# Interleaving the two halves of every moving operand in a two-block transformer kernel

## The chip, the cores and the metric

The kernel runs on one core of a Trainium2 chip. The metric is the device time of one execution in microseconds (us). The engines that matter here are TensorE (PE in the profile, with PEld for its weight loads), VectorE (DVE), ScalarE (ACT), GpSimd (POOL) and SyncE (SP), which issues the transfers.

## What is computed

Two transformer blocks in a row act on one sequence of 256 tokens of width 2048, all in float32. The first block has two kinds of attention and a feed-forward part with a short convolution:

```python
h = rmsnorm(x, pre_mix_g)
proj = h @ w_in                                   # 2048 -> 4368
o_a = swa_sink_attention(q_a, k_a, v_a, sinks)    # 16 heads, 2 kv heads, window 128
o_b = forgetting_attention(q_b, k_b, v_b, log_f)  # 16 heads
mix = concat(rmsnorm(o_a), rmsnorm(o_b)) @ w_out  # 2048 -> 2048
x = x + rmsnorm(mix, post_mix_g)
u = causal_dwconv(rmsnorm(x, pre_ffn_g) @ w_up, conv_w, conv_b)   # 2048 -> 11264, 3 taps
gate, val = split(u, 2)
x = x + rmsnorm((gelu(gate) * val) @ w_down, post_ffn_g)          # 5632 -> 2048
```

The second block modulates its norms by a condition vector (`w_ada`, 2048 to 12288), projects the sequence and a context of 256 tokens, runs windowed attention and pooling, and ends with `square(relu(hm @ w_mlp_up)) @ w_mlp_down` (2048 to 8192 and back) and a last norm. The weights, some 485 MB by the page's HBM reads, are read once.

## The kernel before

Every product of activations and weights is made of three matmuls. A weight tile arrives by DMA (`raw`), ACT copies it to a rounded part `hi` (line 160), DVE writes the remainder `lo = raw - hi` (line 172), and the activations are held as `hi` and `lo` in the same way. `products` (line 294) then issues hi·hi, hi·lo and lo·hi into one PSUM bank.

Two shapes of matmul carry nearly all the work. In form A the weights are the stationary operand (128 columns) and the transposed activations x^T are the moving operand, 256 columns: the output has features on the partitions. The groups v (first part), kva, qa, qk, q, up and mup read x^T that `make_ht` has written into tiles of `xt_tile` (line 367), 192 bytes past the start of a tile of 8,448 bytes. In form B the activations are stationary and 512 columns of weights move (groups wo_a, wo_b, wo_p, dn, mdn, u; 352 and 336 columns in v; 256 in kv and ckv). Counted over the program, line 294 issues 9,312 matmuls of 256 columns, 3,552 of 512 and 288 of 352 or 336.

A group is one weight matrix slice: `run` walks its blocks, each of two half-blocks. A half-block is 24 matmuls of 256 columns or 12 of 512. `hi` and `lo` have four tiles each, so ACT and DVE can be at most four half-blocks ahead. Other DVE and ACT work is written between half-blocks, at `tick`: the reading of finished PSUM banks (`after`), attention (`sides`), and the sums over `w_ada` (`fill`). The order on each engine is then set by the scheduler of the framework from this text. After an up group, `taps` reads the banks for the convolution: one ACT and two DVE instructions for each of 8 slices of 256 columns, spread over the ticks of the group that follows. Groups run up0, up1, up2, then dn (both halves), up3, up4, dn and so on; later mup and mdn alternate.

Two kinds of extra matmul stand in the program. `LEAD` names 15 groups in which one short matmul (64 rows, 128 columns, line 289) goes ahead of a block's first product; its output is overwritten or not used. `warm_mix` (line 344) fills TensorE while the norm between two parts is worked out by ACT and DVE, ahead of up0 and of mup0: five matmuls each of several read patterns of one operand, all with 512 columns: in a row (`plain`), every second column, two halves in turn (`turns(2)`, columns 0, 256, 1, 257, ...), four parts 128 columns apart in turn (`turns(4)`, also 512), and others.

Of the kernel before, what the change touches and what calls it, by code (L numbers as in the profile page):

```python
# [9 lines left out]
F32R = mybir.dt.float32r  # L10
# [62 lines left out]
class Kernel:  # L73
# [204 lines left out]
    def products(self, bank, prog, w, x, first, last):  # L278
        nc = self.nc
        (wh, wl), (xh, xl) = w, x  # L280
        for n, op in enumerate(prog):
            passes = ((wh, xh), (wh, xl), (wl, xh))
            for m, (ww, xx) in enumerate(passes):
# [7 lines left out]
                else:  # L291
                    _, o, w_, tt, c = op
                    dst, lhsT, rhs = bank[:, o:o + w_], xx[:, 128 * tt:128 * tt + 128], ww[:, c:c + w_]
# [35 lines left out]
    def warm_mix(self, kind, after, x):  # L329

        bk = self.bank("warm")
        x = x.rearrange("p k t -> p (k t)")
        one = self.ones.bitcast(mybir.dt.bfloat16)
        plain, every2, every4 = x[:, 0:512], x[:, 0:1024:2], x[:, 0:2048:4]
        turns = lambda n: x[:, 0:512].rearrange("p (a b) -> p b a", a=n)
        w, flat = x[:, 1024:1152], x[:, 1024:1025].to_broadcast([128, 128])
        same = x[:, 0:2].rearrange("p (o n) -> p o n", o=1).broadcast_to([128, 256, 2])
        kinds = (((one[:, 0:128], one.rearrange("p (o n) -> p o n", o=1).broadcast_to([128, 2, 256])), (w, plain), (w, every2), (w, same), (flat, plain),
                  (w, turns(2))), ((w, every4), (w, turns(16)), (w, turns(4))))[kind]
        with self.tc.issue_after(after.ins):  # L340
            for lhsT, rhs in kinds:
                out = bk if len(rhs.shape) == 2 else bk.rearrange("p (a b) -> p a b", b=rhs.shape[-1])
                for _ in range(5):
                    self.pe.matmul(out, lhsT, rhs, start=True, stop=True, skip_group_check=True)
# [298 lines left out]
    def main(self):  # L643
# [82 lines left out]
        st = {}  # L726
# [3 lines left out]
        def v_after(banks):  # L730
            st["vb"] = vb = [self.P4([128, 1024]) for _ in range(2)]
            f = self.const("f", [128, 32])
            for tt in range(2):
                self.dve.tensor_tensor(out=f[:, 16 * tt:16 * tt + 16], in0=banks[3 * tt + 2][:, 320:336],
                                        in1=heads[:, 0:16], op=ALU.add)
            for tt in range(2):
                for c, w in enumerate((352, 352, 320)):
                    dst, src = vb[tt][:, 352 * c:352 * c + w], banks[3 * tt + c][:, 0:w]
                    if (tt + c) % 2:
                        self.dve.tensor_copy(out=dst, in_=src)  # L740
                    else:
                        ac.copy(dst, src)
# [51 lines left out]
        def kva_after(banks):  # L794
            st["kva"] = kva = self.P4([128, 1024])
            ac.copy(kva[:, 256:512], banks[0][:, 256:512])
            self.dve.tensor_copy(out=kva[:, 0:256], in_=banks[0][:, 0:256])
# [23 lines left out]
        def qa_after(banks):  # L821
            st["qa"] = qa = [self.P4([128, 4, 256]) for _ in range(2)]
            copy_out(pairs(qa), banks)
# [26 lines left out]
        def qk_group(part):  # L850
            def after(banks):
                st["qk", part] = qk = [self.P4([128, 4, 256]) for _ in range(2)]
                copy_out(pairs(qk), banks)
# [17 lines left out]
        def wo_a(half):  # L871
# [9 lines left out]
            def after(banks):  # L881
                for tt in range(2):
                    for c in range(2):
                        dst = st["m"][tt][:, 1024 * half + 512 * c:1024 * half + 512 * c + 512]
                        r = st["ra"][:, tt:tt + 1]
                        ac.activation(dst, banks[2 * tt + c], AF.Copy, scale=r)
# [35 lines left out]
        def wo_b(half):  # L922
# [11 lines left out]
            def done(n, bank):  # L934
# [3 lines left out]
                self.dve.scalar_tensor_tensor(out=m, in0=bank, scalar=st["rb"][:, tt:tt + 1], in1=m,  # L938
# [18 lines left out]
        def up(g):  # L957
            def after(banks):
# [4 lines left out]
                def taps(s, i):  # L963
                    if not gv:
# [30 lines left out]
        def accumulate(y, bank, n, half, first):  # L995
            tt, c = divmod(n, 2)
            d = y[tt][:, 1024 * half + 512 * c:1024 * half + 512 * c + 512]
            if first:
                ac.copy(d, bank)
# [529 lines left out]
```

## Time and profile before

| | us |
|---|---|
| median of 3 runs | 2121.12 |
| lowest, highest | 2119.36, 2122.55 |
| the profiled execution, own time | 2122.08 |
| its span from first to last instruction | 2120.3 |
| PE busy / DVE busy / ACT busy in it | 2096.9 / 1576.0 / 1079.0 |

Busy time of PE counts a matmul until its modelled end, and matmuls overlap, so 99% busy does not mean that PE streams at its best rate. The rate is the distance between the starts of matmuls that follow each other. In the chain of waits a piece such as "x864" is a stretch in which one matmul follows the other, and its time divided by its count is that distance.

### The profile page before, as it was taken

Reading aid. Unit: us, or ns where it says so; the run is one execution under the profiler, and the core shown is the slowest. Engines: PE = TensorE matmul, PEld = TensorE weight load, DVE = VectorE, ACT = ScalarE, POOL = GpSimd, SP = SyncE. Lnnn points to the kernel's source line nnn. Section 1 sums busy time; section 2 is a strip of 40 time slices with the busy share of each in tenths; the row PEclk is TensorE's granted clock in tenths of the full one; section 3 lists DMA queues with packets and bytes.
Section 4 is the critical chain, followed back from the end, with each engine's and each line's share of the span. In section 5 each row is a group of like instructions: output and inputs, shape, how many; then the busy total and the mean of one; then the engine's idle time right before and its main releaser. Section 6 shows DMA issues by size and latency. Waiting matters only on the chain.

```text
span 2120.3 us, 34973 instructions
## 1 busy us (share of the span) xinstructions
PE 2096.9 (99%) x14314; PEld 1902.6 (90%) x14314; DVE 1576.0 (74%) x2094; ACT 1079.0 (51%) x1557; POOL 40.3 (2%) x58
## 2 busy tenths in 40 slices
PE   8999999999999999999999999999999999999997
PEld 7998977999998999989989978889898998989986
DVE  6777688888678787897899788765656667555476
ACT  5446565555444553544566476454543434434343
POOL 0001000000000000000000000000000000000000
PEclk9999999999999999999999999999999999999999
DMA  8753576566667788787878754845667677555572
GB/s 308 270 185 138 154 222 240 213 250 233 257 235 263 254 295 307 283 316 277 303 278 276 275 174 144 218 159 181 248 211 275 207 262 249 193 199 183 196 238 100
DMA packets 120960, 491.39 MB, mean 232 GB/s; under 512 B 8736, under 2 KB 12640, under 8 KB 107360
## 3 DMA queue, kind: packets, MB, share of 16 engines
q1 hardware_dynamic: 120800, 489.16, 66.8%
q8 instruction: 112, 1.84, 0.3%
q14 instruction: 48, 0.39, 0.1%
HBM read 484.90 MB, written 2.13 MB: 230 GB/s over the span
## 4 chain that ended last, share of the span: by engine, by line
PE 94%; DVE 3%; DMA 1%; ACT 1%; issue 0%; POOL 0%; SPq 0%; POOLq 0%; ACTq 0%; DVEq 0%
PE b_up L294 23%; PE b_mup L294 17%; PE b_mdn L294 16%; PE b_dn L294 10%; PE b_qk L294 4%; PE b_wo_a L294 4%; PE b_v L294 2%; PE b_u L294 2%; PE b_wo_p L294 2%; PE b_qa L294 2%; PE b_q L294 2%; PE b_wo_b L294 2%; DVE lo L172 1%; PE b_aux L1228 1%; PE b_aux L1185 1%; PE b_aux L1214 1%
## 5 line engine op out<-in xcount | busy, mean ns | idle before, releaser
L172 DVE TENSOR_TENSOR lo<-raw,hi 128x1024 fp32r<-128x1024 f32 (+2 forms) x716 | 849.5, 1199 | 404.2 <-ACT hi L160 401.1
L160 ACT CAST hi<-raw 128x1024 fp32r<-128x1024 f32 (+2 forms) x716 | 731.2, 1031 | 816.1 <-PE b_up L294 206.7
L294 PE MATMUL b_up<-a,hi 128*128 128x256 f32 x2816 | 484.5, 277 | 0.0
L294 PEld LDWEIGHTS b_up<-a,hi 128*128 128x128 f32 x2816 | 425.3, 188 | 0.5
L294 PE MATMUL b_up<-a,lo 128*128 128x256 f32 x1408 | 390.1, 277 | 0.0
L294 PE MATMUL b_mup<-a,hi 128*128 128x256 f32 x2048 | 352.7, 278 | 1.2 <-ACT a L400 1.2
L294 PE MATMUL b_mdn<-hi,p 128*128 128x512 f32 x1024 | 315.5, 389 | 0.0
L294 PEld LDWEIGHTS b_mup<-a,hi 128*128 128x128 f32 x2048 | 309.0, 188 | 1.9 <-ACT a L400 1.5
L294 PE MATMUL b_mup<-a,lo 128*128 128x256 f32 x1024 | 283.5, 277 | 0.0
L294 PEld LDWEIGHTS b_up<-a,lo 128*128 128x128 f32 x1408 | 264.3, 188 | 0.1
L613 DVE SCALAR_TENSOR_TENSOR raw<-raw,srow 128x2048 f32<-128x2048 f32 x96 | 219.6, 2287 | 38.2 <-DMA raw<-in_w_ada 37.8
L294 PEld LDWEIGHTS b_mdn<-hi,p 128*128 128x128 f32 x1024 | 191.7, 188 | 39.4
L294 PE MATMUL b_dn<-hi,p 128*128 128x512 f32 x704 | 217.1, 390 | 0.0
L294 PE MATMUL b_mdn<-lo,p 128*128 128x512 f32 x512 | 199.2, 389 | 0.0
L294 PEld LDWEIGHTS b_mup<-a,lo 128*128 128x128 f32 x1024 | 193.0, 188 | 0.0
L294 PEld LDWEIGHTS b_dn<-hi,p 128*128 128x128 f32 x704 | 131.6, 188 | 26.9
L294 PE MATMUL b_dn<-lo,p 128*128 128x512 f32 x352 | 137.1, 390 | 0.0
L294 PEld LDWEIGHTS b_mdn<-lo,p 128*128 128x128 f32 x512 | 96.1, 188 | 20.0
L294 PE MATMUL b_qk<-a,hi 128*128 128x256 f32 x512 | 92.6, 283 | 0.0
L610 DVE SCALAR_TENSOR_TENSOR p<-raw,srow 128x2048 bf16<-128x2048 f32 x32 | 73.3, 2290 | 15.4 <-DMA raw<-in_w_ada 15.3
L294 PE MATMUL b_wo_a<-hi,a 128*128 128x512 f32 x256 | 80.3, 395 | 0.0
L294 PEld LDWEIGHTS b_qk<-a,hi 128*128 128x128 f32 x512 | 77.5, 188 | 2.8 <-issue 2.0
(276 smaller groups left out, 2527.4 us busy)
## 6 DMA issues: line engine op xcount, KB each, us to landing
raw<-in_w_ada SPq DMA_DIRECT2D x96, 1024.0 KB, 5.9
raw<-in_w_up SPq DMA_DIRECT2D x88, 1024.0 KB, 4.9
raw<-in_w_mlp_up SPq DMA_DIRECT2D x64, 1024.0 KB, 4.9
raw<-in_w_mlp_down SPq DMA_DIRECT2D x64, 1024.0 KB, 5.5
raw<-in_w_in SPq DMA_DIRECT2D x50, 1024.0 KB, 5.8
raw<-in_w_down SPq DMA_DIRECT2D x44, 1024.0 KB, 6.2
raw<-in_w_out SPq DMA_DIRECT2D x32, 512.0 KB, 6.7
raw<-in_w_out SPq DMA_DIRECT2D x16, 1024.0 KB, 6.6
```

The costliest lines, as they stand in the source:

```text
L160: nc.scalar.copy(h, r)
L172: self.dve.tensor_tensor(out=l, in0=r, in1=h.bitcast(F32), op=ALU.subtract)
L294: self.mm = self.pe.matmul(dst, lhsT, rhs, start=first and n == 0 and m == 0, stop=last and n == len(prog) - 1 and m == 2, skip_group_chec ...
L610: self.dve.scalar_tensor_tensor(out=junk, in0=r, scalar=1.0, in1=self.srow[1], op0=ALU.mult, op1=ALU.mult, accum_out=self.adac[:, f:f + 1])
L613: self.dve.scalar_tensor_tensor(out=r, in0=r, scalar=1.0, in1=self.srow[0], op0=ALU.mult, op1=ALU.mult, accum_out=self.ada[:, f:f + 1])
L1185: self.pe.matmul(bk.rearrange("p (m c) -> p m c", m=2), qq, k.rearrange("p (m c) -> p m c", m=2)[:, :, o:o + 256], start=n == 0, stop=n == ...
L1214: self.pe.transpose(bk[:, 128 * m:128 * m + 128], z[:, 128 * m:128 * m + 128], self.ident)
L1228: self.pe.matmul(o[64 * s:64 * s + 64, 128 * qt:128 * qt + 128], v[:, c:c + 64], PT[x][:, 128 * kt:128 * kt + 128], start=kt == 0, stop=kt ...
```

## The change

Every moving operand of `products` is read as two halves in turn: `halves` turns columns 0..n-1 into 0, n/2, 1, n/2+1, and so on. The output is written to PSUM in the order in which columns come (`turns` leaves it contiguous), so a bank now holds its columns interleaved. Whoever reads a bank puts them back by reading every second element (`evens`, `evens2`) into rows (`rows2`, `rows4`): the copies after v, kva, qa, qk, q, u, ckv and kv, the scaling after wo_a, wo_b, wo_p, the convolution, and the sums of dn and mdn. After mup the squares are taken in bank order and the two splits read every second element from SBUF. x^T starts at the start of its tile. `LEAD` is empty. `warm_mix` issues ten matmuls each of six and of three patterns with 256 columns, all in two streams at other distances.

```diff
-LEAD = dict(qa=2, qk0=0, qk1=0, up0=6, up3=0, up5=0, up7=0, up9=0, q=0, mup2=0, mup3=0, mup4=0, mup5=0, mup6=0, mup7=0)
+LEAD = {}
+def halves(ap):
+    return ap.rearrange("p (a b) -> p b a", a=2)
+def turns(ap):
+    return ap.rearrange("p (b a) -> p b a", a=2)
+def evens(ap):
+    return ap.rearrange("p (b a) -> p a b", a=2)
+def rows2(ap):
+    return ap.rearrange("p (a b) -> p a b", a=2)
...
+                dst, rhs = turns(dst), halves(rhs)
                 self.mm = self.pe.matmul(dst, lhsT, rhs, start=first and n == 0 and m == 0,
...
-        kinds = (((one[:, 0:128], one.rearrange("p (o n) -> p o n", o=1).broadcast_to([128, 2, 256])), (w, plain), (w, every2), (w, same), (flat, plain),
-                  (w, turns(2))), ((w, every4), (w, turns(16)), (w, turns(4))))[kind]
+        at = lambda o, d: x[:, o:o + 2 * d].rearrange("p (a b) -> p b a", a=2)[:, 0:128]
+        kinds = (((w, at(0, 128)), (w, at(0, 256)), (w, at(16, 128)), (w, at(48, 128)), (w, at(0, 512)), (x[:, 1024:1280:2], at(0, 128))),
+                 ((w, at(8, 128)), (w, at(0, 136)), (w, at(0, 192))))[kind]
...
-        return self.A8([128, 2112], F32R)[:, 48:48 + 2048].rearrange("p (k t) -> p k t", t=256)
+        return self.A8([128, 2112], F32R)[:, 0:2048].rearrange("p (k t) -> p k t", t=256)
...
-                    ac.activation(d, p, AF.Identity, scale=cw(t, 2), bias=cw(t, 3))
-                    self.dve.scalar_tensor_tensor(out=d[:, 1:256], in0=p[:, 0:255], scalar=cw(t, 1), in1=d[:, 1:256],
-                                                  op0=ALU.mult, op1=ALU.add)
-                    self.dve.scalar_tensor_tensor(out=d[:, 2:256], in0=p[:, 0:254], scalar=cw(t, 0), in1=d[:, 2:256],
-                                                  op0=ALU.mult, op1=ALU.add)
+                    ac.activation(rows2(d), evens(p), AF.Identity, scale=cw(t, 2), bias=cw(t, 3))
+                    for n in (1, 2):
+                        o = rows2(d)[:, :, n:128]
+                        self.dve.scalar_tensor_tensor(out=o, in0=evens(p)[:, :, 0:128 - n], scalar=cw(t, 2 - n), in1=o,
+                                                      op0=ALU.mult, op1=ALU.add)
+                        o = d[:, 128:128 + n]
+                        self.dve.scalar_tensor_tensor(out=o, in0=evens(p)[:, 0, 128 - n:128], scalar=cw(t, 2 - n), in1=o,
+                                                      op0=ALU.mult, op1=ALU.add)
...
-                self.dve.tensor_tensor(out=d, in0=bank, in1=d, op=ALU.add)
+                self.dve.tensor_tensor(out=rows2(d), in0=evens(bank), in1=rows2(d), op=ALU.add)
```

On PE, where up3 follows the first dn pair, the kernel before has these rows (line 294 is `products`, line 289 the short matmul):

```order
L294 MATMUL b_dn_5670<-hi_5746,p_745_5201 128x512
L294 MATMUL b_dn_5670<-hi_5746,p_746_5202 128x512
L294 MATMUL b_dn_5670<-lo_5764,p_745_5201 128x512
L289 MATMUL b_up_5820<-a_603_3882,hi_5768 128x128
L294 MATMUL b_up_5820<-a_603_3882,hi_5768 128x256
L294 MATMUL b_up_5820<-a_604_3883,hi_5768 128x256
```

and the changed kernel these at the same place (line 326 is `products`):

```order
L326 MATMUL b_dn_5744<-hi_5820,p_743_5259 128x512
L326 MATMUL b_dn_5744<-hi_5820,p_744_5260 128x512
L326 MATMUL b_dn_5744<-lo_5838,p_743_5259 128x512
L326 MATMUL b_up_5894<-a_602_3910,hi_5842 128x256
L326 MATMUL b_up_5894<-a_603_3911,hi_5842 128x256
```

The short matmul is gone, and the products stand in the same order with outputs of the same size.

On DVE, in the first ticks of the first dn group, the kernel before applies the taps of up1 like this between two `lo` remainders (line 172):

```order
L970 SCALAR_TENSOR_TENSOR p_732_5030<-b_up_4455,vecs,p_732_5030 128x255
L172 TENSOR_TENSOR lo_4997<-raw_4816,hi_4965 128x1024
L172 TENSOR_TENSOR lo_4999<-raw_4816,hi_4967 128x1024
L972 SCALAR_TENSOR_TENSOR p_732_5030<-b_up_4455,vecs,p_732_5030 128x254
L970 SCALAR_TENSOR_TENSOR p_731_5029<-b_up_4453,vecs,p_731_5029 128x255
L970 SCALAR_TENSOR_TENSOR p_731_5029<-b_up_4454,vecs,p_731_5029 128x255
L172 TENSOR_TENSOR lo_5037<-raw_4879,hi_5003 128x1024
```

and the changed kernel like this (line 202 is the remainder):

```order
L202 TENSOR_TENSOR lo_5041<-raw_4858,hi_5009 128x1024
L1009 SCALAR_TENSOR_TENSOR p_730_5072<-b_up_4481,vecs,p_730_5072 128x2
L1009 SCALAR_TENSOR_TENSOR p_729_5071<-b_up_4479,vecs,p_729_5071 128x1
L1006 SCALAR_TENSOR_TENSOR p_729_5071<-b_up_4479,vecs,p_729_5071 128x2x126
L1009 SCALAR_TENSOR_TENSOR p_729_5071<-b_up_4479,vecs,p_729_5071 128x2
L1009 SCALAR_TENSOR_TENSOR p_729_5071<-b_up_4480,vecs,p_729_5071 128x2
L202 TENSOR_TENSOR lo_5083<-raw_4921,hi_5045 128x1024
```

Each tap is now one instruction over two runs and a second one over the one or two columns at the seam of the halves, and more of them stand between two remainders.

## Rows read from the trace of the kernel before

**Rows 1.** The page, part 4: the chain that ended last, shares by engine.

```profile
PE 94%; DVE 3%; DMA 1%; ACT 1%; issue 0%; POOL 0%; SPq 0%; POOLq 0%; ACTq 0%; DVEq 0%
```

**Rows 2.** Chain of waits, pieces in time: start us, length us, engine, tile, line, count.

```profile
48.04 17.04 PE b_v L294 x108
122.21 3.02 PE b_qk L294 x24
...
408.99 101.96 PE b_up L294 x864
510.95 43.56 PE b_dn L294 x192
554.76 87.25 PE b_up L294 x768
...
1434.97 62.19 PE b_mup L294 x528
```

**Rows 3.** Timeline of PE before up0: start us, length us, what, count [idle before].

```profile
363.67 0.40 PE L344 MATMUL b_warm<-a 128*128 128x512 f32 x1
...
364.60 0.61 PE L344 MATMUL b_warm<-a 128*128 128x512 f32 x1
...
366.39 0.64 PE L344 MATMUL b_warm<-a 128*128 128x512 f32 x1
...
369.11 0.38 PE L344 MATMUL b_warm<-a 128*128 128x512 f32 x1
...
369.97 0.38 PE L344 MATMUL b_warm<-a 128*128 128x512 f32 x1
...
370.19 0.27 PE L383 MATMUL b_aux<-ident,a 128*128 128x128 f32 x1
```

**Rows 4.** Timeline before mup0: the norm on DVE, weight loads of `turns(4)`, transposes.

```profile
1400.05 1.02 DVE L459 TENSOR_SCALAR a<-a,sm 128x512 f32<-128x512 f32 x2 [0.75 <-POOL sm L441]
...
1400.90 1.03 PEld L344 LDWEIGHTS b_warm<-a 128*128 128x128 f32 x4 [0.23 <-issue]
...
1402.31 0.49 PE L383 MATMUL b_aux<-ident,a 128*128 128x128 f32 x3
```

**Rows 5.** Timeline of PE where up3 follows dn, with a short matmul.

```profile
554.12 0.39 PE L294 MATMUL b_dn<-lo,p 128*128 128x512 f32 x1
554.44 0.32 PE L289 MATMUL b_up<-a,hi 64*128 64x128 f32 x1
554.70 0.50 PE L294 MATMUL b_up<-a,hi 128*128 128x256 f32 x2
```

**Rows 6.** Windows: stretch, us, busy time (count) by engine, PEclk, DMA share, GB/s.

```profile
642.00:685.00 43.00, 43.00 (x192) 35.58 (x191) 42.18 (x53) 20.69 (x26) 0.00 (x0) 1.00 0.76 268
685.00:773.00 88.00, 88.00 (x773) 87.58 (x772) 66.05 (x74) 44.81 (x57) 0.54 (x1) 1.00 0.75 268
773.00:816.00 43.00, 43.00 (x192) 35.59 (x191) 40.45 (x51) 21.10 (x26) 0.00 (x0) 1.00 0.86 304
...
1035.00:1104.00 69.00, 68.95 (x320) 56.93 (x320) 64.98 (x92) 45.03 (x73) 1.40 (x2) 1.00 0.83 298
1104.00:1129.00 25.00, 24.58 (x210) 24.21 (x209) 24.33 (x37) 21.35 (x40) 3.51 (x3) 1.00 0.65 227
```

**Rows 7.** Groups of DVE by shape: count | busy us, mean ns of one | idle before.

```profile
L972 DVE SCALAR_TENSOR_TENSOR p<-b_up,vecs,p 128x254 f32<-128x254 f32 x88 | 40.7, 475 | 0.0
L970 DVE SCALAR_TENSOR_TENSOR p<-b_up,vecs,p 128x255 f32<-128x255 f32 x88 | 40.0, 475 | 0.4 <-ACT p L969 0.2
...
L1001 DVE TENSOR_TENSOR a<-b_dn,a 128x512 f32<-128x512 f32 x32 | 21.2, 685 | 0.6 <-PE b_dn L294 0.6
...
L734 DVE TENSOR_TENSOR f<-b_v,heads 128x16 f32<-128x16 f32 x2 | 0.3, 172 | 0.2 <-PE b_v L294 0.2
```

**Rows 8.** Waits of PE (total us, times, longest), and a window at the start.

```profile
PE b_aux L383 <- DVE a L459: 1.5, 1, 1.5
...
17.00:20.30 3.30, 3.30 (x13) 3.08 (x12) 3.30 (x4) 1.75 (x2) 0.00 (x0) 0.50 1.00 394
```

More of the change, by code (lines that the diff above doesn't have):

```diff
@@ L332, in warm_mix @@
         x = x.rearrange("p k t -> p (k t)")
[L333 to L337, printed above, removed]
-        kinds = (((one[:, 0:128], one.rearrange("p (o n) -> p o n", o=1).broadcast_to([128, 2, 256])), (w, plain), (w, every2), (w, same), (flat, plain),
-                  (w, turns(2))), ((w, every4), (w, turns(16)), (w, turns(4))))[kind]
+        w = x[:, 1024:1152]
+        at = lambda o, d: x[:, o:o + 2 * d].rearrange("p (a b) -> p b a", a=2)[:, 0:128]
+        kinds = (((w, at(0, 128)), (w, at(0, 256)), (w, at(16, 128)), (w, at(48, 128)), (w, at(0, 512)), (x[:, 1024:1280:2], at(0, 128))),
+                 ((w, at(8, 128)), (w, at(0, 136)), (w, at(0, 192))))[kind]
         with self.tc.issue_after(after.ins):
             for lhsT, rhs in kinds:
-                out = bk if len(rhs.shape) == 2 else bk.rearrange("p (a b) -> p a b", b=rhs.shape[-1])
-                for _ in range(5):
-                    self.pe.matmul(out, lhsT, rhs, start=True, stop=True, skip_group_check=True)
+                for _ in range(10):
+                    self.pe.matmul(turns(bk[:, 0:256]), lhsT, rhs, start=True, stop=True, skip_group_check=True)
     def preload(self, func, after):
@@ L733, in v_after @@
             for tt in range(2):
-                self.dve.tensor_tensor(out=f[:, 16 * tt:16 * tt + 16], in0=banks[3 * tt + 2][:, 320:336],
+                self.dve.tensor_tensor(out=f[:, 16 * tt:16 * tt + 16], in0=evens(banks[3 * tt + 2][:, 0:336])[:, 1, 152:168],
                                         in1=heads[:, 0:16], op=ALU.add)
             for tt in range(2):
[L737 to L740, printed above, removed]
-                    else:
-                        ac.copy(dst, src)
+                for c in range(3):
+                    if c < 2:
+                        pieces = [(rows2(vb[tt][:, 352 * c:352 * c + 352]), evens(banks[3 * tt + c][:, 0:352]))]
+                    else:
+                        e = evens(banks[3 * tt + c][:, 0:336])
+                        pieces = [(vb[tt][:, 704:872], e[:, 0]), (vb[tt][:, 872:1024], e[:, 1, 0:152])]
+                    for dst, src in pieces:
+                        if (tt + c) % 2:
+                            self.dve.tensor_copy(out=dst, in_=src)
+                        else:
+                            ac.copy(dst, src)
             self.sides.append(decay(f))
@@ L795, in kva_after @@
             st["kva"] = kva = self.P4([128, 1024])
-            ac.copy(kva[:, 256:512], banks[0][:, 256:512])
-            self.dve.tensor_copy(out=kva[:, 0:256], in_=banks[0][:, 0:256])
+            ac.copy(rows2(kva[:, 256:512]), evens(banks[0][:, 256:512]))
+            self.dve.tensor_copy(out=rows2(kva[:, 0:256]), in_=evens(banks[0][:, 0:256]))
             def turn():
@@ L822, in qa_after @@
             st["qa"] = qa = [self.P4([128, 4, 256]) for _ in range(2)]
-            copy_out(pairs(qa), banks)
+            copy_out([rows4(t) for t in pairs(qa)], [evens2(b) for b in banks])
         def qa_conv(d, r):
@@ L852, in after @@
                 st["qk", part] = qk = [self.P4([128, 4, 256]) for _ in range(2)]
-                copy_out(pairs(qk), banks)
+                copy_out([rows4(t) for t in pairs(qk)], [evens2(b) for b in banks])
             return Group(f"qk{part}", 16, 1024, self.loader(w_in, 0, 1280 + 1024 * part, 1024), a_banks(8), xs, after=after, side=swa if part == 0 else lambda: fox(0))
@@ L1136, in kv_after @@
             r = self.P2(512)
[L1137 to L1138 removed]
+            ac.copy(rows4(r), evens2(banks[0]))
+            self.dve.tensor_copy(out=st["v2"][:, 0:512].rearrange("p (t a b) -> p t a b", t=2, a=2),
+                                 in_=banks[1].rearrange("p (t b a) -> p t a b", t=2, a=2))
             rope(r, [k[:, 0:512] for k in st["kk"]], [k[:, 0:512] for k in st["kl"]])
@@ L1147, in q_after @@
             st["qr"] = [self.P2(512) for _ in range(4)]
-            copy_out(st["qr"], banks)
+            copy_out([rows4(t) for t in st["qr"]], [evens2(b) for b in banks])
         def q_conv(d, r):
@@ L1253, in u_after @@
             st["u"] = u = [self.P4([128, 1024]) for _ in range(2)]
-            copy_out([u[tt][:, 512 * c:512 * c + 512] for tt in range(2) for c in range(2)], banks)
+            copy_out([rows2(u[tt][:, 512 * c:512 * c + 512]) for tt in range(2) for c in range(2)], [evens(b) for b in banks])
         def u_before():
```

32 lines of the change are left out of this document (18 added, 14 removed).

## The prediction

> **What bounds the kernel now.** I read the chain of waits first: 94% of the span belongs to PE [rows 1]. Then its pieces, because a busy PE need not stream at its best rate. Length over count gives the pitch, the distance between the starts of two matmuls. With 256 columns it is 87.25/768 = 113.6 ns after dn and 101.96/864 = 118.0 ns in up0 to up2, 62.19/528 = 117.8 ns in mup0 and mup1; with 512 columns 43.56/192 = 226.9 ns; in v 17.04/108 = 157.8 ns [rows 2]. So the same instruction has two pitches, and the reader should ask what the floor is.
>
> The fill ahead of up0 answers that, for it runs several read patterns of one operand, 512 columns each, five times [rows 3]. Columns in a row go from 363.67 to 364.60 in four matmuls: 232 ns each. Every second column goes from 364.60 to 366.39 in four: 448 ns. Two halves in turn go from 369.11 to 369.97 in four: 215 ns. [...] The fill ahead of mup0 adds four parts 128 columns apart in turn: five matmuls from 1400.90 to 1402.31, 282 ns each [rows 4]. What limits PE in most of the kernel is thus how fast it reads the moving operand, by 5%; next to it stands DVE, which in some stretches is nearly full: 42.18 of 43 us and 40.45 of 43 us in two dn pairs, 89.3 of 94 us from 1035 to 1129 [rows 6].
>
> **The change part by part.** *512 columns.* The halves are 256 columns apart, just the pattern that ran at 215 ns. 3,552 matmuls by (226.9 - 215.3) = **-41 us**. All of it lies on the chain.
>
> *256 columns.* Here the halves of x^T are 128 columns apart, and no row shows that pattern. [...] I take 109 ns, because the number of streams is two as in the 215 ns row. Of the 9,312 matmuls 1,392 are in the two stretches at 118 ns, 5,856 in up3 to up10, mup2 to mup7, q and kva, which I price with the row at 113.6, and 2,064 in the rest, between 113.6 and 3.02/24 = 125.8 ns with its interruptions [rows 2], for which I take 117. That is 1,392 x 9 + 5,856 x 4.6 + 2,064 x 8 = 12.5 + 26.9 + 16.5 = 56 us; some 4 us of it are pauses at the start of a block that stay, so **-52 us**. The new start of x^T I price at nothing by itself: the operand of the fill also began at the start of its tile.
>
> *v.* 288 matmuls of 352 and 336 columns, two to one, at 157.8 ns, floor (2 x 148.7 + 142)/3 = 146.5 ns: **-3 us**.
>
> *Short matmuls.* The last dn matmul and the short one are 0.32 us apart, where 0.227 is the pitch, and 0.26 us follow to the first product [rows 5]. Without it one of the two pauses stays, so 0.09 + 0.26 = 0.35 us go, 15 times: **-5 us**. But the groups that follow a short matmul are the ones at 113.6 ns, and up1, up2 and mup1, which have none, run at 118. If the read were still short of the floor, dropping them would put all 9,312 at 118; at the floor there is nothing left to lose, and the 215 ns row is at the floor.
>
> *Fills.* Ahead of mup0 the norm ends at 1400.05 + 1.02 = 1401.07, and the transposes that need it start at 1402.31, behind the fill [rows 4]. Its 30 matmuls at 109 ns, 3.3 us, are over before, so the 1.2 us between go: **-1 us**. Ahead of up0 the fill now has 24 matmuls in 6.5 us from 363.67 to 370.19 [rows 3] and six before; 60 at 109 ns are 6.5 us in all, some 1.3 us shorter. But there PE already waits 1.5 us for the norm [rows 8], so nothing is won and the idle time grows to 2.8 us. [...]
>
> *DVE.* Each of the 88 + 88 taps gets a second, tiny instruction at the seam [rows 7]. The smallest DVE instruction that reads PSUM took 172 ns; a tap of 255 columns took 475 ns [rows 7], which bounds it from above; I take 0.19 us, the low end being the near one, so 176 x 0.19 = 33 us over the kernel. What is queued behind them is the next `lo`, and PE waits for that. In the dn pairs (16 tiny ones each, 3.0 us) PE's time falls to 192 x 215.3 = 41.3 us. The pair from 642 then has 42.18 + 3.0 = 45.2 us of DVE work (3.9 over), that from 773 has 43.5 (2.2 over). From 1035 to 1129 PE falls by 288 matmuls x 11.6 and 192 x 6, 4.5 us, to 89.5, and DVE rises to 92.3 (2.8 over). I charge all of it, **+9 us**, though the four `lo` tiles may cover a part. The up pairs have room: 66.05 of 88 us [rows 6].
>
> *Reading banks at a step of two.* DVE and ACT now read every second element. No row shows DVE or ACT with such a step; PE's row at a step of two costs 448 against 232. So the bounds are nothing and a doubling; a gain is excluded, as the same elements are read. I take nothing, because DVE handles one column in about 1 ns (the 255 columns add some 0.3 us to the 172 ns of the smallest) while PE at its full rate asks for one in 0.42 ns. The doubling is the second rival.
>
> *The rest.* ckv gets one ACT copy more and v two pieces more; ACT is busy for 21.35 of 25 us there [rows 6], the k tiles are used in attention much later, and PE does not wait for them. SP's order differs only there, four small copies behind one load; their user comes later too. No cost.
>
> Sum: -41 - 52 - 3 - 5 - 1 + 9 = -93 us. From the profiled execution's own 2122.1 us that is 2029; that execution was 1 us above the median, so 2028. DVE does not only lag in the stretches shown, so I round up to **2032 us**.
>
> [...] What the rows show is that a read which changes between two places at every column is the fastest of all, 215 ns [rows 3], while a step of two or many streams is slow. [...]
>
> **The rivals.**
> *First, x^T gains nothing by turning.* Either the distance of 128 columns or the weight load is the limit: form A needs a load of 128 columns for each 109 ns. For it: 113.6 ns at 256 columns is nearer to its floor than 226.9 at 512. Against it: three transposes, each with a load of its own, followed each other at (0.49 - 0.27)/2 = 0.11 us [rows 3, 4], so loads keep that pace. With no short matmuls all would then run at 118: 9,312 x 118 = 1,099 against 1,072 us now (164 + 665 + 242), +27, with -41 - 3 - 5 - 1 and some +7 for DVE: about **2106 us** (2064 if they hold 113.6).
>
> *Second, a step of two slows DVE.* Doubled, a tap costs 475 ns more and an accumulation 685. In the 131 us from 685 to 816, DVE has 66.05 + 40.45 = 106.5 us; 32 taps and 8 accumulations add 20.7 us, the tiny ones 6.1: 133.3 us against PE's 83.7 + 41.3 = 125.0. DVE would then set the pace of up and dn, 8 us lost in each of the four periods and about as much again in up0 to up2 and near 1100: +50 us, 2082. With half the penalty the up pairs still have room and only dn loses, +20 us. I put it at **2067 us** (2050 to 2085). For it: DVE's load; against it: nothing in this trace, either way. [...]
>
> *Third, slower.* Two places 128 columns apart collide, as in the row of four: 141 ns. 9,312 x 141 = 1,313 us, +241, less 50 for the rest, no DVE charge as PE is slow: about **2313 us**. It decides from a pitch of about 120.5 ns, where the 50 us saved elsewhere are used up. For it: the 282 ns row is the only one with that distance. Against it: four streams, not two, and the 448 ns row says that more places at once is what costs. [...]
>
> That the change does not do what it says is ruled out by the order of the built program: all products stand as before, the short ones are gone.
>
> **How the numbers follow.** The forecast has 62%, the second rival 14%, the first 13%, the third 8%, and 3% are left for something unseen, transfers among them (DMA share 0.86 in a dn pair, which would become 0.90 [rows 6]). Its own range is 2016 (DVE's excess covered by its tiles, 2% rounding) to 2050. The range of 2016 to 2090 takes in the forecast, the second rival and a part of the first. A measurement can tell about 0.2% of this kernel from no change. Faster by more: 62 + 14 + 12 + 1 = 89%; slower by more: 8 + 1 = 9%; the rest 2%.
>
> **What would show it.** The chain's pieces: up and mup at 108 to 110 ns, alike in all groups, dn and mdn at 215 to 217, v at 147. The fill with `at(0, 128)` beside `at(0, 256)` shows the distance by itself. Taps at 475 ns and accumulations at 685 clear the second rival; tiny taps near 0.19 us and small waits of PE for `lo` in dn show the DVE term. Up groups at 118 mean the first rival, over 120 the third.

## The result and the profile after

The changed kernel takes **2074.16 us** (median of four runs, 2072.93 to 2075.81) against 2121.58 us for the kernel before in the same measurement: ratio 0.9778, 95% interval 0.9761 to 0.9795. That is 47 us less. The direction was as forecast and the time lies in the range of 2016 to 2090, but outside the forecast's own range of 2016 to 2050: only about half of the forecast gain of 90 us came.

The page of the changed kernel, first its span, then busy time and share of each engine, then the chain of waits by engine, which answers [rows 1]:

```profile
span 2072.9 us, 35204 instructions
...
PE 2030.2 (98%) x14344; PEld 1885.6 (91%) x14344; DVE 1594.8 (77%) x2271; ACT 1078.6 (52%) x1559; POOL 40.4 (2%) x58
...
PE 85%; DVE 8%; DMA 3%; ACT 2%; issue 2%; POOL 0%; POOLq 0%; ACTq 0%; SPq 0%; DVEq 0%
```

PE's share of the chain fell from 94% to 85%; VectorE (DVE) now holds 8% and transfers 3%, mostly those of w_ada. So the kernel has become a little less a kernel of one engine. The chain's pieces answer [rows 2] (start us, length us, engine, tile, line, count):

```profile
47.49 15.87 PE b_v L326 x108
...
133.97 2.68 PE b_qk L326 x24
...
394.48 101.84 PE b_up L326 x912
...
928.48 85.76 PE b_up L326 x768
...
1472.80 41.44 PE b_mdn L326 x192
1514.24 42.88 PE b_mup L326 x384
```

Length over count is the pitch. With 512 columns it is 41.44/192 = 215.8 ns, with 352 and 336 columns 146.9 ns, both as forecast. With 256 columns it is 101.84/912 = 85.76/768 = 42.88/384 = **111.7 ns**, alike in every group: the two levels of [rows 2] are gone, but the one that took their place is not 109.

The waits of PE (us in total, times, longest us; the wait for the input at the start is left out):

```profile
PE b_dn L326 <- DVE lo L202: 10.6, 8, 3.1
...
PE b_aux L411 <- DVE a L487: 3.5, 2, 2.8
PE b_ckv L326 <- DVE lo L202: 2.0, 1, 2.0
```

The first line is new: before, PE did not wait for `lo` in the dn groups. The 2.8 us of the second are the idle time ahead of up0 that the prediction expected.

To see where 47 us came from I added up the distances between the starts of PE's records, and counted what a distance exceeds the pitch by, when that is over 25 ns, as a pause:

| | forecast us | measured us |
|---|---|---|
| products of 512 columns, without pauses | -41 | -40.2 |
| products of 256 columns, without pauses | -52 | -24.8 |
| products of 352 and 336 columns, without pauses | -3 | -3.2 |
| rest of PE (short matmuls, fills, attention) | -6 | -3.2 |
| pauses between products | +9 | +23.7 |
| sum | -93 | -47.7 (spans: -47.4) |

Two terms failed: the pitch of 256 columns (27 us) and the pauses (15 us). Of the 23.7 us, 18.3 lie in the 512-column groups. The experiments are about these two.

### The profile page after: what moved, and what is told of

It is laid out like the page before. It is cut to its first block, busy times and chain, and to the rows that moved or that the text cites. A ratio compares the mean times of both kernels' runs of the same rounds, so it can differ in the third digit from the quotient of the medians.

```text
span 2072.9 us, 35204 instructions
## 1 busy us (share of the span) xinstructions
PE 2030.2 (98%) x14344; PEld 1885.6 (91%) x14344; DVE 1594.8 (77%) x2271; ACT 1078.6 (52%) x1559; POOL 40.4 (2%) x58
## 4 chain that ended last, share of the span: by engine, by line
PE 85%; DVE 8%; DMA 3%; ACT 2%; issue 2%; POOL 0%; POOLq 0%; ACTq 0%; SPq 0%; DVEq 0%
PE b_up L326 21%; PE b_mup L326 17%; PE b_mdn L326 16%; PE b_dn L326 5%; PE b_qk L326 4%; PE b_wo_a L326 4%; DVE lo L202 3%; PE b_v L326 2%; DMA raw<-in_w_ada 2%; PE b_qa L326 2%; PE b_q L326 2%; PE b_wo_p L326 2%; PE b_wo_b L326 2%; PE b_u L326 1%; DVE raw L641 1%
## 5 line engine op out<-in xcount | busy, mean ns | idle before, releaser
L326 PE MATMUL b_up<-a,hi 128*128 128x256 f32 x2816 | 473.7, 276 | 0.0
L326 PE MATMUL b_mup<-a,hi 128*128 128x256 f32 x2048 | 344.4, 275 | 1.3 <-ACT a L428 1.3
L326 PE MATMUL b_mdn<-hi,p 128*128 128x512 f32 x1024 | 304.7, 379 | 0.0
L326 PEld LDWEIGHTS b_up<-a,lo 128*128 128x128 f32 x1408 | 270.5, 192 | 0.0
L326 PE MATMUL b_dn<-hi,p 128*128 128x512 f32 x704 | 210.9, 383 | 0.0
L326 PE MATMUL b_mdn<-lo,p 128*128 128x512 f32 x512 | 194.0, 379 | 0.0
L326 PEld LDWEIGHTS b_dn<-hi,p 128*128 128x128 f32 x704 | 133.9, 191 | 18.8
L326 PE MATMUL b_dn<-lo,p 128*128 128x512 f32 x352 | 134.9, 386 | 10.6 <-DVE lo L202 10.6
L326 PEld LDWEIGHTS b_dn<-lo,p 128*128 128x128 f32 x352 | 67.1, 191 | 23.8 <-DVE lo L202 14.3
L1006 DVE SCALAR_TENSOR_TENSOR p<-b_up,vecs,p 128x254 f32<-128x254 f32 (+1 forms) x176 | 82.2, 472 | 1.0 <-ACT p L1002 0.9
```

Source lines behind the costliest of these rows:

```text
L326: self.mm = self.pe.matmul(dst, lhsT, rhs, start=first and n == 0 and m == 0, stop=last and n == len(prog) - 1 and m == 2, skip_group_chec ...
L1006: self.dve.scalar_tensor_tensor(out=o, in0=evens(p)[:, :, 0:128 - n], scalar=cw(t, 2 - n), in1=o, op0=ALU.mult, op1=ALU.add)
```

## Experiments on the pitch of 256 columns

**What limits it: the fill.** The fill matmuls feed nothing, so their shapes can be changed freely.

```diff
-        at = lambda o, d: x[:, o:o + 2 * d].rearrange("p (a b) -> p b a", a=2)[:, 0:128]
-        kinds = (((w, at(0, 128)), (w, at(0, 256)), (w, at(16, 128)), (w, at(48, 128)), (w, at(0, 512)), (x[:, 1024:1280:2], at(0, 128))),
-                 ((w, at(8, 128)), (w, at(0, 136)), (w, at(0, 192))))[kind]
+        two = lambda n: x[:, 0:512].rearrange("p (a b) -> p b a", a=2)[:, 0:n // 2]
+        row = lambda n: x[:, 0:n]
+        kinds = (((w, two(256)), (w[:, 0:64], two(256)), (w, two(128)), (w[:, 0:64], two(128)), (w, row(128)), (w, row(256))),
+                 ((w, two(264)), (w, two(384)), (w, two(512))))[kind]
```

> The changed kernel with other fill matmuls, 10 in a row of each kind. Ahead of the first up group: moving two halves in turn of 256 columns against 128 stationary columns; the same against 64 stationary columns; two halves of 128 columns against 128 and against 64 stationary columns; a plain row of 128 and of 256 columns against 128 stationary columns. Ahead of the first mup group: two halves in turn of 264, 384 and 512 columns against 128 stationary columns. They feed nothing. Theory L (at 256 columns the load of 128 stationary columns, about 111.7 ns, is the limit, not the moving stream): 256 columns against 64 stationary ones go to 107 to 109 ns; 128 moving columns stay near 111 against 128 stationary columns and fall well below it (near 60) against 64; 264 columns 111 to 113, 384 columns about 161, 512 columns 215.8. Rival (a fixed cost on each two-halves read): 64 stationary columns leave 111.7 unchanged, 128 moving columns take 57 to 60 against 128 stationary ones, 264 columns take 115.

The table by windows; each window but the sixth runs from the first matmul of one kind to the first of the next, so its length is ten pitches (window, its length in us, busy us and instructions of PE, PEld, DVE, ACT, POOL, granted clock, DMA share, GB/s):

```profile
350.69:351.81 1.12, 1.12 (x12) 1.11 (x11) 1.12 (x3) 1.12 (x5) 0.00 (x0) 1.00 0.00 0
351.81:352.90 1.09, 1.09 (x13) 1.09 (x11) 1.09 (x3) 1.01 (x5) 0.00 (x0) 1.00 0.00 0
352.90:353.96 1.06, 1.06 (x12) 1.06 (x11) 0.79 (x3) 1.06 (x3) 0.00 (x0) 1.00 0.00 0
353.96:354.55 0.59, 0.59 (x13) 0.59 (x12) 0.29 (x3) 0.23 (x2) 0.55 (x1) 1.00 0.00 0
354.55:355.67 1.12, 1.12 (x14) 1.12 (x12) 0.69 (x3) 1.09 (x2) 0.92 (x1) 1.00 0.00 0
355.67:356.85 1.18, 1.18 (x12) 1.18 (x12) 1.18 (x2) 1.18 (x3) 0.00 (x0) 1.00 0.00 0
1376.57:1377.70 1.13, 1.13 (x12) 1.12 (x10) 0.89 (x2) 1.13 (x2) 0.00 (x0) 1.00 0.00 0
1377.70:1379.32 1.62, 1.62 (x12) 1.62 (x11) 0.60 (x2) 1.62 (x4) 0.00 (x0) 1.00 0.00 0
1379.32:1381.48 2.16, 2.16 (x12) 1.85 (x11) 1.38 (x5) 1.73 (x2) 0.54 (x1) 1.00 0.00 0
```

Row 1 is the kernel's own case, but with halves 256 and not 128 columns apart: 256 columns in two halves against 128 stationary columns, 112 ns. Row 2 halves only the stationary columns: 109 ns, the value that I had forecast. Rows 3 and 4 say it louder: 128 moving columns take 112 ns against 128 stationary ones (the first of the ten, behind a matmul against 64, some 55 ns: 1.06 us less nine of 111.7 ns) and 59 ns against 64. Row 5 does the same with a plain row of columns: 112 again, so the halves have nothing to do with it. From 264 columns up (113, 162, 216 ns) the moving side sets the pitch. In these rows the pitch is thus the longer of two things: the moving columns at about 0.42 ns each (216/512), or the load of 128 stationary columns, **111.7 ns**. At 256 columns the change has brought the first below the second. Row 6, a plain row of 256, has 118 ns between the starts of its second and its tenth matmul (the first takes 170, and the next work starts only at 356.90, behind the window), the upper of the two levels before. The changed kernel's own fill bears the load out: its sixth kind moves the same columns as its first, against a stationary operand read at a step of two, and takes 1.19 us for ten where the first takes 1.11.

One thing does not fit a load that always takes 111.7 ns. Transposes also have a load of 128 columns each; in the kernel before, twelve in a row ahead of mup0 are

```profile
1402.31 1.47 PE L383 MATMUL b_aux<-ident,a 128*128 128x128 f32 x12
```

With 0.27 us for a single one [rows 3] that is (1.47 - 0.27)/11 = 0.109 us each, and in the changed kernel the median distance between their starts is 109 ns too. So 111.7 ns is what these products need against 128 stationary columns; why transposes follow each other faster no run shows.

**The same in place.** Two of the three products of each 256-column group load half of their stationary columns, which leaves out the correction products of the upper 64 rows.

```diff
+                if op[0] == "A" and m:
+                    dst, lhsT = dst[0:64], lhsT[:, 0:64]
                 dst, rhs = turns(dst), halves(rhs)
```

> The changed kernel, where two of the three products of each 256-column group load only 64 of their 128 stationary columns: the correction products of the upper 64 rows are left out. Moving columns, instruction count and everything else stay. Theory L: the pitch of these 6,208 matmuls falls from 111.7 to 109.2 as in the fill, the other 3,104 keep 111.7 or lie between: 6,208 x 2.5 ns = -15, 2074 - 15 = about 2059, if TensorE's waits stay as they are; VectorE becomes later against a faster TensorE, so up to 2064. Rival (the pitch of the real groups is not the load but a cost of the two-halves read or of PSUM): 2072 to 2076, pitch 111.7 for all.

Pieces of its chain of waits:

```profile
669.38 84.48 PE b_up L328 x768
...
1512.41 42.24 PE b_mup L328 x384
```

The pitch is 84.48/768 = 110.0 ns, just (111.7 + 2 x 109.2)/3. So the load theory holds in the real groups, and the 256-column products without pauses took some 15 us less than in the second run of the changed kernel. The time did not follow: 2070.19 us (2068.87 to 2078.26) against 2074.87 (2073.63 to 2077.18) for the changed kernel on the same chip, runs that overlap, where 2059 to 2064 was expected. In the profiled executions the span is 5.4 us shorter, and the pauses behind products of 512 and 256 columns grew by 8.0 us, 5.2 of them at 512. That a faster PE runs into DVE fits this, but one profile does not show it: from the first run of the changed kernel to the second the pauses at 512 columns alone differ by 3.8 us.

**The short matmuls.** They were left out of the kernel before, alone, and put back into the changed kernel, alone.

```diff
-LEAD = dict(qa=2, qk0=0, qk1=0, up0=6, up3=0, up5=0, up7=0, up9=0, q=0, mup2=0, mup3=0, mup4=0, mup5=0, mup6=0, mup7=0)
+LEAD = {}
```

> The kernel before with nothing changed but that the 15 short leading matmuls are left out. Theory: the 256-column pitch of the kernel before has two levels, 113.3 and 118 ns, and the leads set the lower one: without them the led groups (about 13 groups of 384 matmuls and a few smaller) go to 118, 384 x 13 x 4.7 ns = +23, less 15 x 0.35 = 5 for the leads: about 2135 to 2142. Rival (leads do nothing for the pace): 2116.

The kernel before without them took 2138.57 us (2138.10 to 2139.08; ratio 1.0072, 1.0057 to 1.0087), as expected. Pieces of its chain:

```profile
403.10 103.37 PE b_up L294 x912
550.01 90.45 PE b_up L294 x768
...
1549.83 45.23 PE b_mup L294 x384
```

The last two are 117.8 ns, in groups that stood at 113.6 [rows 2]. There the leads did set the lower level before, as I had read it. But the first line went the other way: 103.37/912 = 113.3 ns in up0 to up2, which stood at 118.0 behind the one lead in up0 [rows 2]. A lead moves a group from one level to the other, and not always down.

> The changed kernel with the 15 short leading matmuls put back, nothing else. Theory L: there is one level of the 256-column pitch, 111.7, which a lead cannot lower, so the leads only cost their own 15 x 0.1 to 0.35: 2075 to 2080. Rival (a lower level near 109 exists and the leads would set it, as they do in the kernel before): led groups at 109, 13 x 384 x 2.7 ns = -13, 2061 to 2064.

With the leads put back the changed kernel took 2080.25 us (2077.04 to 2081.28; ratio 0.9802, 0.9787 to 0.9817). Two pieces of its chain:

```profile
1476.02 41.44 PE b_mdn L326 x192
1517.72 43.07 PE b_mup L326 x384
```

The mup group is 0.2 us longer than without a lead (42.88), so its pitch is no lower, and it starts 0.26 us behind the end of mdn (1476.02 + 41.44 = 1517.46), where the lead stands. The leads have nothing left to win and cost 0.45 us in this group; over the kernel it is some 0.4 us each (2080.25 - 2074.16 = 6.1 us for 15).

**The offset of x^T.**

```diff
-        return self.A8([128, 2112], F32R)[:, 0:2048].rearrange("p (k t) -> p k t", t=256)
+        return self.A8([128, 2112], F32R)[:, 48:48 + 2048].rearrange("p (k t) -> p k t", t=256)
```

> The changed kernel with x^T put back at 192 bytes past a multiple of 256, nothing else. Theory L: the fill of the changed kernel shows one pitch for halves at every offset and distance, so the 256-column pitch stays 111.7 and the time 2073 to 2075. Rival (the offset is what makes two halves in turn run at their best): 9,312 matmuls at 113.3 or more, 2088 or more.

It took 2076.95 us (2071.59 to 2081.20; ratio 0.9781, 0.9763 to 0.9799), with mup groups of 42.88 us as in the changed kernel. The offset is worth nothing measurable, as assumed. Its profile shows more waits in dn than the changed kernel's (17.1 against 10.6 us); but a second run of the changed kernel itself has 13.9, so these vary from run to run.

## Experiments on the pauses

**Each half of the change alone.** First only the moving weights (512, 352 and 336 columns, and the 256 of kv and ckv) in halves, on top of the kernel before; then only x^T in halves, its offset, the seam instructions and no leads, with wide weights in a plain row.

```diff
-                    dst, lhsT, rhs = bank[:, o:o + w_], xx[:, 128 * tt:128 * tt + 128], ww[:, c:c + w_]
+                    dst, lhsT, rhs = turns(bank[:, o:o + w_]), xx[:, 128 * tt:128 * tt + 128], halves(ww[:, c:c + w_])
```

> The kernel before, with one part of the change: the weights that move as 512 (or 352, 336, 512-wide v) columns are read from two halves in turn and their products put back in order when PSUM is read. x^T as the moving side (256 columns), its offset and the short leading matmuls stay as before. Theory L+D (the 512-column gain is whole, and what was lost lies in the 256-column pace and in VectorE): pitch of 512 columns 215.8 ns, of 256 columns 113.3 and 118 as before, 2121 - 40 - 2 = about 2079 to 2084, few waits of TensorE on the lo split since the seam instructions are not there. Rival (the faster 512-column stream itself runs into the lo split or the weight DMA in the dn groups): the down groups show waits as in the changed kernel and the time is 2090 to 2095.

It took 2095.75 us (2088.91 to 2099.40; ratio 0.9868, 0.9844 to 0.9891). The time is just above that of the rival, but the rival's mechanism is not there: PE waits 1.5 us for `lo` in dn, and the pauses at 512 columns grew by 5 us only. Half of what was missing is in the other products. Pieces of its chain:

```profile
545.23 87.25 PE b_up L324 x768
...
674.18 90.58 PE b_up L324 x768
```

The second stands at the upper level, 117.9 ns, where the kernel before has 87.25 us and the same lead. The 256-column products took 7 us more without pauses. Why a lead does not take hold there stays open; a plain row of 256 columns has two levels here (113.6 and 118 ns), and a change elsewhere moved this group from one to the other.

```diff
-                dst, rhs = turns(dst), halves(rhs)
+                if op[0] == "A":
+                    dst, rhs = turns(dst), halves(rhs)
```

> The other part alone: x^T as the moving side is read from two halves in turn, x^T at a multiple of 256 bytes, no leading matmuls, seam instructions on VectorE; the 512-column weights move in a plain row as before. Theory L+D: pitch of 256 columns 111.7 ns everywhere, of 512 columns 226.9 as before; the 256-column sum falls by 25, the leads give 5, the waits on the lo split in the dn groups are small since these run at the old pace (about 5): 2121 - 25 = about 2094 to 2099. Rival (the seam instructions alone make the waits, whatever the pace of the 512 columns): 2102 to 2108, with waits of 10 us or more on the lo split. If the two parts simply add, this and the wide part alone sum to the -47 of the whole.

It took 2107.77 us (2105.90 to 2109.57; ratio 0.9927, 0.9912 to 0.9942): the rival's time. PE's wait in dn, with the wide weights at their old pitch:

```profile
PE b_dn L327 <- DVE lo L202: 9.9, 7, 4.0
```

The seam instructions and the faster x^T groups make the waits without any help from the wide weights. Both halves together give -27 - 15 = -42 us, near the -47 of the whole.

**The seam instructions taken away.** Once simply left out, then made needless: x^T of the up and mup groups is stored with its even tokens first and its odd tokens behind, by reading the transposes' PSUM at a step of two, so that taking turns gives the tokens in their order.

```diff
-                        o = d[:, 128:128 + n]
-                        self.dve.scalar_tensor_tensor(out=o, in0=evens(p)[:, 0, 128 - n:128], scalar=cw(t, 2 - n), in1=o,
-                                                      op0=ALU.mult, op1=ALU.add)
```

> The changed kernel without the 176 seam instructions on VectorE: the first one or two tokens of the second 128 get no convolution taps from the tokens ahead of them. Nothing takes their place. Theory D: 36 us of VectorE less, the waits of TensorE on the lo split in the dn groups shrink by most of their 10.6 us and the half-clock stretches behind them go: 2056 to 2062. Rival (the waits do not come from VectorE's load): 2070 to 2074.

```diff
-                    e0 = nc.scalar.activation(h[:, f], p, AF.Copy, scale=g)
-                    e1 = self.dve.scalar_tensor_tensor(out=l[:, f], in0=p, scalar=g, in1=h[:, f].bitcast(F32),
+                    e0 = nc.scalar.activation(one(h[:, f]), pick(p), AF.Copy, scale=g)
+                    e1 = self.dve.scalar_tensor_tensor(out=one(l[:, f]), in0=pick(p), scalar=g, in1=one(h[:, f].bitcast(F32)),
...
-            ht["need"], ht["xs"], _ = self.make_ht(lambda tt, k: m[tt][:, 128 * k:128 * k + 128], self.vec("pre_ffn", 0, 16))
+            ht["need"], ht["xs"], _ = self.make_ht(lambda tt, k: m[tt][:, 128 * k:128 * k + 128], self.vec("pre_ffn", 0, 16), apart=True)
```

(`one` and `pick` are `rows2` and `evens` where `apart` is set; the taps and the split of mup are those of the kernel before; the gain and shift path of mup is changed in the same way.)

> The changed kernel, with the x^T of the up and mup groups stored with its even tokens in the first 128 columns and its odd tokens in the second, by reading the transposes' PSUM at a step of two, so that taking turns gives the tokens in their natural order: no seam instructions (176 x 0.207 = 36 us of VectorE less), taps and the split of mup in plain order as in the kernel before. Everything else is the changed kernel. Theory D (seam instructions make the lo split late in the dn groups, TensorE waits and then runs at half clock for some matmuls): the waits on the lo split in dn fall from 10.6 to 3 us or less and the 512-column breaks fall from 26 to about 10: 2074 - 15 to 20 = 2054 to 2060. Rival (waits there come from the faster TensorE itself, the weight DMA or ScalarE): 2068 to 2074, waits as in the changed kernel. Pitch of 256 columns stays 111.7 in both.

> The changed kernel with x^T of up and mup stored as even and odd tokens, so without seam instructions, once more and with more rounds, beside the changed kernel on one chip: 2056 to 2062, ratio to the kernel before 0.970 to 0.972, 12 to 15 us under the changed kernel.

> The changed kernel itself once more, beside the others of this call on one chip: 2070 to 2077. Its second profile tells how far the waits on the lo split differ from one execution to the next; if they are made by a fixed order on VectorE, they stand at the same five places (near 513, 644, 773, 902, 1032 us) with lengths of 0.8 to 5 us.

Left out, so that the first one or two tokens of the second 128 lack taps: 2062.35 us (2058.37 to 2066.43; ratio 0.9720, 0.9701 to 0.9739). Made needless: 2059.97 us (2056.42 to 2062.99; ratio 0.9701, 0.9687 to 0.9716), and again, on one chip with the changed kernel, **2060.66** us (2058.52 to 2062.32; ratio 0.9714, 0.9699 to 0.9728) against 2074.87 us (2073.63 to 2077.18). So the seams cost 12 to 14 us, and the version with x^T apart beats both kernels: it takes 60 us from the kernel before. PE's waits in dn, made needless and its second run:

```profile
PE b_dn L326 <- DVE lo L202: 1.6, 2, 1.4
```

```profile
PE b_dn L326 <- DVE lo L202: 3.1, 5, 1.2
```

With the seams left out and the rest as changed it is 6.3 us, less than the 10.6 and 13.9 of the changed kernel, more than expected. The longest of them, 2.8 us, has another cause. DVE in that kernel, ahead of the wait (start us, length us, line, what, [idle before, released by]):

```profile
917.59 2.29 DVE L641 SCALAR_TENSOR_TENSOR raw<-raw,srow 128x2048 f32<-128x2048 f32 x1 [2.81 <-DMA raw<-in_w_ada]
...
919.81 2.35 DVE L202 TENSOR_TENSOR lo<-raw,hi 128x1024 fp32r<-128x1024 f32 x2
```

DVE stood 2.81 us for a piece of w_ada, with the `lo` that PE needed queued behind it. The rival, the transfer of w_ada, thus has a share, in some waits. Nor is it gone with the seams: in the second run with x^T apart it still holds 2.2% of the chain.

**How a wait comes about.** DVE in the changed kernel around the start of the first dn group, at 496.32 us:

```profile
491.60 2.29 DVE L638 SCALAR_TENSOR_TENSOR p<-raw,srow 128x2048 bf16<-128x2048 f32 x1 [1.53 <-DMA raw<-in_w_ada]
...
494.95 2.28 DVE L641 SCALAR_TENSOR_TENSOR raw<-raw,srow 128x2048 f32<-128x2048 f32 x1
...
498.30 0.47 DVE L1006 SCALAR_TENSOR_TENSOR p<-b_up,vecs,p 128x254 f32<-128x254 f32 x1
498.69 0.20 DVE L1009 SCALAR_TENSOR_TENSOR p<-b_up,vecs,p 128x1 f32<-128x1 f32 x1
...
512.23 2.28 DVE L638 SCALAR_TENSOR_TENSOR p<-raw,srow 128x2048 bf16<-128x2048 f32 x1
514.43 0.08 DVE L638 DVE_READ_ACCUMULATOR p<-raw,srow 128x1 f32 x1
514.43 1.22 DVE L202 TENSOR_TENSOR lo<-raw,hi 128x1024 fp32r<-128x1024 f32 x1
```

The first tap stands at 498.30, 2.0 us behind the start of dn. In the kernel before it stands ahead of dn, which starts at 510.95 [rows 2]:

```profile
508.49 0.87 DVE L970 SCALAR_TENSOR_TENSOR p<-b_up,vecs,p 128x255 f32<-128x255 f32 x2
```

In the changed kernel DVE is a queue from its first tap on: 16 taps, 16 seams, 5 `lo`, and the multiply for w_ada at 512.23, 15.9 us behind the start of dn; before, the same multiply came 519.26 - 510.95 = 8.3 us behind it, and with x^T apart 10.4. The `lo` that comes after it starts at 514.43, and PE waits until 515.7. In the second run of the changed kernel PE waits at the same five places, near 513, 643, 773, 901 and 1036 us, for 1.4 to 5.0 us, as one order on DVE in every run would make them. The longest, near 1036 us, has more ahead of it in the first run: DVE stood 0.43 us for POOL and 0.88 us for ACT there. A wait can have a second price. PE in the longest one (start us, length us, what, count, [idle before]), and two windows around it:

```profile
1035.93 0.79 PE L326 MATMUL b_dn<-lo,p 128*128 128x512 f32 x1 [3.13 <-DVE lo L202]
1036.52 1.06 PE L326 MATMUL b_dn<-hi,p 128*128 128x512 f32 x2
1037.37 0.63 PE L326 MATMUL b_dn<-lo,p 128*128 128x512 f32 x1
```

```profile
1032.00:1036.00 4.00, 0.87 (x5) 0.44 (x3) 3.12 (x7) 3.99 (x5) 0.00 (x0) 0.95 0.79 244
1036.00:1039.00 3.00, 3.00 (x7) 2.44 (x8) 2.57 (x4) 2.94 (x4) 0.00 (x0) 0.50 0.71 224
```

After the pause of 3.13 us the granted clock is 0.50, and two matmuls take 1037.37 - 1036.52 = 0.85 us, 425 ns each, until about 1039. In the whole kernel 13 matmuls of 512 columns ran so, behind the two longest waits in dn; at 0.21 us more each that is 2.7 us. Not every wait brings this: behind the 2.8 us in the kernel with the seams left out the granted clock stayed at 1.00,

```profile
921.00:924.00 3.00, 2.91 (x14) 2.56 (x14) 2.90 (x4) 0.00 (x0) 0.00 (x0) 1.00 0.84 315
```

and behind 1.9 us at 513 us in the second run of the changed kernel no matmul was slow, where the first run has seven. What decides it no run shows.

**The multiply moved.** One multiply for w_ada goes from the first half of each dn group to the second.

```diff
-PACE.update({f"dn{i}{half}": ((5, 8), (2, 5, 8))[half] for i in range(0, 10, 2) for half in range(2)})
+PACE.update({f"dn{i}{half}": ((8,), (2, 4, 6, 8))[half] for i in range(0, 10, 2) for half in range(2)})
```

> The changed kernel, with one w_ada multiply of 2.28 us moved on VectorE: out of the first half of each dn group (tick 5, right behind the bunch of taps and seam instructions) into the second half (ticks 2, 4, 6, 8 in place of 2, 5, 8). The same work in all. Theory D (VectorE's load in the first half of dn, taps with seams plus this multiply, makes the lo split late there): the waits near 513, 644, 773, 902 and 1032 us fall by up to 2 us each, the waits on lo in dn from 10.6 to 4 or less, time 2064 to 2069. Rival (the waits go where the multiply goes, or come from the transfer of w_ada): waits as long in the second half, 2072 to 2078.

PE's largest waits behind the one for the input:

```profile
PE b_aux L411 <- DVE a L487: 4.1, 3, 2.8
PE b_aux L411 <- DVE p L425: 4.0, 2, 2.7
PE b_dn L326 <- DVE lo L202: 3.9, 5, 1.3
```

The waits in dn fell to 3.9 us, as the theory wanted, and the pauses at 512 columns from 30.2 in the second run of the changed kernel to 18.1. The time, 2072.78 us (2069.91 to 2074.32), is 2 us below the changed kernel beside it, and their runs overlap: not the 2064 to 2069 expected, but the rival's 2072 to 2078. The profile is of the fastest of the four runs. New waits at the transposes (4.0 us) and 3.5 us more pauses at 256 columns took most of it back. Moving DVE's work moves the waits, as the rival had it; taking it away, as with x^T apart, removes most of them.

## Why the prediction was half right

*Right: 512 columns and v.* Pitches of 215.8 and 146.9 ns against 215.3 and 146.5; the 215 ns of [rows 3] were the right yardstick, and 40.2 of 41 us came. No row shows the 148.7 and 142 ns behind the 146.5 of v, which were my estimate; the changed kernel has 149 ns between the starts at 352 columns and 142.5 at 336.

*Right: no pitch level is left for a short matmul to set.* The two runs with leads taken out and put back show it. The saving was priced at 0.35 us each; put back, they cost some 0.4. That the level before came from the leads was half true: in up0 to up2 a lead stood where the level rose.

*Wrong: 109 ns as the floor of 256 columns.* I bounded the pitch by the moving stream alone, and used the 0.11 us between transposes [rows 4] to argue against the weight load as the limit. The transposes do keep 109 ns, but they say nothing of the products: against 128 stationary columns these follow each other every 111.7 ns here, and with 64 every 109.2. No run shows 109 ns for products of 256 columns against 128 stationary ones; the runs showed 111.7 in its place, and 2.7 ns x 9,312 = 25 us. The first rival named this limit but priced it at no gain; the truth lay between. The 141 ns of the third rival, for halves 128 columns apart, was never near: the changed kernel's own fill ran distances of 128, 136, 192, 256 and 512 columns at 111.7 alike. Nor did the distance matter with half the load: 109.2 ns with halves 128 columns apart (in place) and 109 with 256 (row 2 of the fill).

*Wrong in size: DVE, +9 against +23.7.* The instructions were priced too high and their effect too low. A seam instruction shows 207 to 209 ns, but they overlap their neighbours: the next DVE instruction starts 0.13 us after (498.69 to 498.82), and DVE's busy time rose by 18.8 us in all, not 33. Groups of DVE in the changed kernel and, last, one in the kernel before (line, shapes, count, busy us, mean ns):

```profile
L1006 DVE SCALAR_TENSOR_TENSOR p<-b_up,vecs,p 128x254 f32<-128x254 f32 x88 | 41.4, 473 | 1.0 <-ACT p L1002 0.9
...
L1038 DVE TENSOR_TENSOR a<-b_dn,a 128x512 f32<-128x512 f32 x32 | 21.0, 680 | 0.0
...
L1009 DVE SCALAR_TENSOR_TENSOR p<-b_up,vecs,p 128x1 f32<-128x1 f32 x88 | 18.2, 207 | 0.0
...
L1412 DVE TENSOR_TENSOR p<-p,p 128x512 fp32r<-128x512 f32 x32 | 25.8, 809 | 7.9 <-ACT p L1411 7.9
```

```profile
L1372 DVE TENSOR_TENSOR p<-p,p 128x512 fp32r<-128x512 f32 x32 | 21.9, 688 | 5.1 <-ACT p L1371 4.8
```

The step that failed is comparing DVE's load with PE's time over a whole dn pair: DVE was busy for 41.00 of 43 us in the pair from 757 us, not more than PE has, and PE still lost some 1.7 us there. Several long waits come within the pair, where DVE has fallen behind at its start and the taps, the seams and a multiply stand ahead of one `lo`; and behind some of them comes the halved clock. Against the 15 us too little, x^T apart gives back 14. What waits are left then, for w_ada among others, was not taken apart.

That the time lies in the range of 2016 to 2090 is luck: the part of it where 2074 lies was there for the second rival (2050 to 2085), whose mechanism did not make the time.

*The second rival* is refuted for PSUM: taps took 473 ns against 475 and accumulations 680 against 685 [rows 7]. It is real for SBUF, in a place that I had not looked at: the split of mup reads its SBUF operand at a step of two, and takes 809 ns on DVE where the kernel before took 688, with 829 against 620 on ACT. PE did not wait for it in mup. The third rival, slower, had nothing behind it.

## What to carry to other kernels

A matmul's pitch here had two floors, the moving columns and the stationary load; measure both, each by itself, before pricing a faster stream, and where one operand's tile is 128 x 128 and the other 256 wide they nearly meet (109.2 and 111.7 ns). When the engine that bounds a kernel becomes faster by some per cent, look at each place where another engine was only just ahead, in the order of that engine's queue and not by its load over a stretch. If a layout can give the order that a consumer wants at no cost (here PSUM read at a step of two, once; a tap that reads it so took 473 ns against 475), put it there and not into small instructions on the fullest engine.

## What the runs showed of the hardware

- Against 128 stationary columns products of 128 and of 256 moving columns alike follow each other every 111.7 ns; with 64 stationary columns 128 moving ones take 59 ns and 256 take 109. Transposes, each with a load of 128 columns, keep 109.
- Two halves in turn run at 215.8 ns for 512 columns. With 256 columns against 128 stationary ones neither the distance of the halves (128 to 512 columns) nor their offset (0 to 48 columns) changed the pitch of 111.7 ns.
- DVE and ACT read PSUM at a step of two as fast as in a row (a tap 473 against 475 ns on DVE, 563 against 563 on ACT); in SBUF a step of two cost DVE 0.24 ns a column (809 against 688 ns).
- Behind a pause of PE of 3.13 us the granted clock, 1.00 from 1020 to 1032 us, was 0.50 from 1036 to 1039 us, which cost some 1.3 us more (six matmuls at 0.21 us); behind one of 2.82 us in another kernel it stayed at 1.00.
